# A block of two networks on one core: zeros are multiplied during the first loads, and VectorE adds the first norm's squares

## The chip, the cores and the metric

The kernel runs on one core of a Trainium2 chip. The time is that of the device for one execution, in microseconds (us); of several runs the median is given. A profiled execution also has a span, from the first to the last instruction that the profiler saw.

## The reference, cut to what matters

Input is x with 512 tokens of width 1024, in float32. A first block runs a feed-forward part (ffn1), a token mixer and a second feed-forward part (ffn2); a second block runs two more layers. Only the first part is touched:

```python
def rms_norm(x, g):
    xf = x.astype(jnp.float32)
    y = xf * lax.rsqrt(jnp.mean(xf * xf, axis=-1, keepdims=True) + RMS_EPS)
    return (y * g.astype(jnp.float32)).astype(x.dtype)

def swiglu(x, w_gate, w_up, w_down):
    return (jax.nn.silu(x @ w_gate) * (x @ w_up)) @ w_down

x = x + 0.5 * swiglu(rms_norm(x, ffn1_norm), ffn1_w_gate, ffn1_w_up, ffn1_w_down)
x = x + token_mixer(rms_norm(x, mix_norm), ...)
```

The token mixer holds, beside its products with weights, a recurrence over the tokens that the kernel solves in blocks, with small triangular systems.

## The kernel before, in words

x lies transposed in SBUF: eight tiles `x` of 128 features by 512 tokens. A product in float32 is made of three in the faster type fp32r: each operand is split into a high part and the rest, and `mm3` adds high x high, high x rest and rest x high in one PSUM bank (`pm`). For x the parts are `xh` (ScalarE, with the norm's gain as scale) and `xl` (VectorE), made by `split_scaled`; for a weight tile `raw` of 128 x 1024 they are `wh` (a cast, on ScalarE or VectorE) and `wl` (a subtraction on VectorE), made by `wload`. One weight group against the eight x tiles is 24 matmuls of 128x512. The norm's factor is applied after the product, so TensorE can start before the norm is known.

`rms` first makes the eight pairs of xh and xl, then calls `sumsq`: ScalarE squares each x tile (`sq`, the first into `acc`), and the seven others are added to `acc` one by one, on GpSimd. `fold` sums `acc` over the partitions by two matmuls with a matrix of ones (`rones`, a cast of a part of the constants `cst`), and `rsqrt` makes `rstd` of it, with ScalarE's function Sqrt.

In `ffn`, each of the 22 column groups takes a gate group (`ffn_g`) and an up group (`ffn_u`) of weights. Beside that, `put_low` loads weights of a later part (here `w_in` of the mixer), makes their `wl` and stores it in DRAM (`low`), to be loaded again when it is needed. Every load and store is issued by SyncE, in one queue in order. `raw` has three buffers, `wh` and `wl` four each, so that a load waits until an older one has been split.

The order on every engine is not that of the code. `Rec` records all operations, and `schedule` plans the whole program with a cost per operation, a state of ScalarE's tables, of the buffers and of TensorE's clock; at each moment an engine takes the ready operation with the lowest number, which is its place in the code plus a bias (`late`, 60, for the operations of the norm). An operation that may run on two engines (a cast, some additions) is given to one of them. Any change to the first operations can thus move operations everywhere behind them. `emit` writes the program in the planned order.

In the mixer, `inverse32` solves the small triangular systems of one pair of heads: two stores of `ab` into DRAM (`dab`), eight loads `n` of their diagonal blocks in another layout, 31 steps on VectorE that make `u`, four stores of it (`dtt`), and two loads (`TT`) of the result for TensorE. There are four pairs.

Of the kernel before, what the change touches and what calls it, by code (L numbers as in the profile page):

```python
# [643 lines left out]
class Net:  # L644
    def __init__(self, tc, a, ctx, wbufs=(3, 4, 4), slots=76):
        self.tc, self.a = tc, a
        self.nc = self.rec = Rec(tc.nc)
        self.cp = ctx.enter_context(tc.tile_pool(name="cst", bufs=1))
        self.wp = ctx.enter_context(tc.tile_pool(name="wgt", bufs=1))
        self.wbufs = dict(zip(("raw", "wh", "wl"), wbufs))  # L650
        self.tp = ctx.enter_context(tc.tile_pool(name="act", bufs=1))
        self.sp = ctx.enter_context(tc.tile_pool(name="small", bufs=4))
        self.pm = ctx.enter_context(tc.tile_pool(name="pmm", bufs=8, space=PSUM))
        self.dp = ctx.enter_context(tc.tile_pool(name="dram", bufs=1, space=bass.MemoryType.DRAM))
        self.n = 0
        self.slots = slots
        self.late = 60
        self.low, self.later, self.behind, self.far = {}, [], 40, None
        nc = self.nc
        self.cst = self.cp.tile([128, _NC], F32, name="cst")  # L660
        self.vec = self.cp.tile([128, _NV], F32, name="vec")
        nc.sync.dma_start(out=self.vec, in_=a["vec"])
        self.load_x(a["xT"])
        nc.sync.dma_start(out=self.cst, in_=a["cst"])
        self.ident = self.c("ident")
        self.cr = {}
        for m in ("ones", "bones"):
            self.cr[m] = self.cp.tile([128, 128], F32R, name="r" + m)
            nc.vector.tensor_copy(self.cr[m], self.c(m))
        self.eps6 = self.cst[:, _COFF["eps"]:_COFF["eps"] + 1]  # L670
        self.epsg = self.cst[:, _COFF["eps"] + 1:_COFF["eps"] + 2]
        self.one = self.cst[:, _COFF["eps"] + 3:_COFF["eps"] + 4]
# [128 lines left out]
        self.nc.vector.scalar_tensor_tensor(l, src, g, h.bitcast(F32), op0=ALU.mult, op1=ALU.subtract)  # L801
        return h, l

    def sumsq(self, gains=None):

        nc = self.nc
        acc = self.T(p="acc")
        for k in range(KT):
            if k == 0:
                q = acc  # L810
            else:
                q = self.T(p="sq")
            if gains is None:
                nc.scalar.activation(q, self.x[k], AF.Square)
            else:
                nc.scalar.activation(q, self.x[k], AF.Square, scale=gains(k))
            if k:
                nc.gpsimd.tensor_tensor(acc, acc, q, ALU.add)
        ps = self.P()
        self.fold(ps, "ones", acc)  # L820
        return ps
# [16 lines left out]
        nc.vector.tensor_scalar(r, r, -0.5 * scale, 1.5, op0=ALU.mult, op1=ALU.add)  # L838
        nc.vector.tensor_tensor(out, out, r, ALU.mult)

    def rms(self, gname):

        xs = [self.split_scaled(self.x[k], self.v(gname, k)) for k in range(KT)]
        self.rec.bias = self.late
        ps = self.sumsq()
        rstd = self.T(p="rstd")
        self.rsqrt(rstd, ps, 1.0 / D, 1e-6)
        self.rec.bias = 0
        return xs, rstd


    def ffn(self, n):
        nc = self.nc
        xs, rstd = self.rms(n + "_norm")
        g0 = 0
        for ch, nk in enumerate((8, 8, 6)):
            hs = []
# [852 lines left out]
    def last_norm(self, hf):  # L1710
# [4 lines left out]
        s0 = slice(256 * hf, 256 * hf + 256)  # L1715
        if hf == 0:

            w = self.sm(1, tag="fw", bufs=1)
            o = A.activation(w, self.one, AF.Sqrt)
            o.deps.append(next(p for p in reversed(self.rec.ops[:-1]) if p.table))  # L1720
        acc, q7 = (self.T(shape=(128, 512), p="sq")[:, 0:256] for _ in range(2))
# [31 lines left out]
    def all(self):  # L1753
# [2 lines left out]
        mix = [("w_in", t) for t in (5, 9, 1, 6, 10, 2, 7, 11, 3, 13, 17, 21, 14, 18, 22, 15, 19, 23, *range(26, 42))]  # L1756
        mix += [("w_out_a", h) for h in range(4)] + [("w_out_b", h) for h in range(4)] + [("w_o", g) for g in range(8)]
        n = len(self.rec.ops)
        self.later = mix
        self.ffn("ffn1")  # L1760

        w = [o for o in self.rec.ops[n:] if o.fn == "dma_start"][:2]
        l = [o for o in self.rec.ops[:n] if o.fn == "dma_start"]
# [31 lines left out]
```

## Time and profile before

| what | value |
|---|---|
| median of 3 runs | 1911.29 us (1911.15 to 1913.51) |
| the profiled execution | 1912.9 us |
| its span | 1911.1 us |
| TensorE busy (PE) | 98% |
| VectorE (DVE) | 70% |
| ScalarE (ACT) | 45% |
| GpSimd (POOL) | 13% |

PE is TensorE's matmuls and PEld its loads of weights, SPq is SyncE's queue that issues DMAs. A busy time is a share of the span; matmuls are pipelined and overlap in the records, so the distance between the starts of two of them tells the pace. A timeline row reads: start, duration, engine, line, operation, out<-in, shape, count, and in brackets the idle time before it and what ended that. All operations have one line, that of the function which emits them, so they are told apart by the names of their tiles.

### The profile page before, as it was taken

How to read it: one execution, taken by the hardware profiler on the slowest of the kernel's cores; microseconds unless marked ns; L12 is line 12 of the kernel's file. 1: busy time of each engine (PE TensorE's matmuls, PEld its weight loads, DVE VectorE, ACT ScalarE, POOL GpSimd, SP SyncE). 2: the span in 40 equal slices, each digit the busy share in tenths (PEclk: the TensorE clock that was granted, in tenths of full speed). 3: DMA queues.
4: the chain of work that ended last, by engine and by line, in shares of the span. 5: the costliest groups of instructions: out<-in, count | busy, mean ns of one | idle time of the engine just before them, and what ended most of it. 6: DMA issues, size and time to landing. Idle time of an engine off the chain costs nothing.

```text
span 1911.1 us, 25539 instructions
## 1 busy us (share of the span) xinstructions
PE 1867.3 (98%) x9756; PEld 1548.5 (81%) x9756; DVE 1334.9 (70%) x2173; ACT 852.7 (45%) x1187; POOL 252.5 (13%) x201
## 2 busy tenths in 40 slices
PE   8999999999999999999999999999999999999998
PEld 6878888878877777788788788788899888888887
DVE  7766655568977873567566567865378985899774
ACT  5333423453333422444334334522245554898671
POOL 3101101212121200411001014220000101000001
PEclk9999999999999999999999999999999999999999
DMA  7898884526633533658878774412221225555552
GB/s 257 280 318 287 303 281 158 150 97 203 190 125 111 157 129 118 221 180 297 284 262 295 271 272 131 127 58 73 84 86 45 67 67 198 184 185 204 198 176 100
DMA packets 128810, 345.36 MB, mean 181 GB/s; under 512 B 32304, under 2 KB 44848, under 8 KB 128688
## 3 DMA queue, kind: packets, MB, share of 16 engines
q1 hardware_dynamic: 128688, 343.74, 53.7%
q8 instruction: 76, 1.25, 0.3%
q14 instruction: 46, 0.38, 0.1%
HBM read 280.25 MB, written 63.44 MB: 180 GB/s over the span
## 4 chain that ended last, share of the span: by engine, by line
PE 71%; DVE 11%; DMA 11%; ACT 3%; issue 2%; POOL 1%; SPq 1%; DVEq 0%; ACTq 0%; POOLq 0%
PE pm L551 67%; DVE wl L551 4%; PE pw L551 4%; DMA low<-wl 3%; DMA raw<-o_in 2%; DVE t L551 2%; ACT wh L551 2%; DMA raw<-ffn_d 1%; DMA raw<-ffn_u 1%; DMA raw<-w_in 1%; DVE l L551 1%; DMA n<-dab 1%; DMA raw<-gw 1%; SPq L551 1%; DVE q L551 1%
## 5 line engine op out<-in xcount | busy, mean ns | idle before, releaser
L551 ACT CAST wh<-raw 128x1024 fp32r<-128x1024 f32 (+1 forms) x334 | 347.2, 1041 | 678.6 <-PE pm L551 300.7
L551 PE MATMUL pm<-xh,wh 128*128 128x512 f32 x1488 | 584.0, 393 | 9.6 <-ACT xh L551 8.0
L551 PE MATMUL pm<-xl,wh 128*128 128x512 f32 x1488 | 584.1, 393 | 1.9 <-DVE xl L551 1.9
L551 PE MATMUL pm<-xh,wl 128*128 128x512 f32 x1488 | 582.6, 392 | 1.8 <-DVE wl L551 1.8
L551 DVE TENSOR_TENSOR wl<-raw,wh 128x1024 fp32r<-128x1024 f32 (+1 forms) x303 | 383.0, 1266 | 212.1 <-DMA low<-wl 103.6
L551 PEld LDWEIGHTS pm<-xh,wh 128*128 128x128 f32 x1488 | 280.3, 189 | 69.2 <-ACT xh L551 9.1
L551 PE MATMUL pm<-h,wh 128*128 128x512 f32 (+1 forms) x844 | 321.5, 385 | 10.0 <-ACT h L551 6.8
L551 PEld LDWEIGHTS pm<-xl,wh 128*128 128x128 f32 x1488 | 280.5, 188 | 62.4 <-DVE xl L551 5.0
L551 PEld LDWEIGHTS pm<-xh,wl 128*128 128x128 f32 x1488 | 280.4, 188 | 61.6 <-DVE wl L551 4.3
L551 PE MATMUL pm<-l,wh 128*128 128x512 f32 (+1 forms) x844 | 322.2, 384 | 2.6 <-DVE l L551 2.5
L551 PE MATMUL pm<-h,wl 128*128 128x512 f32 (+1 forms) x844 | 321.4, 383 | 0.0
L551 POOL TENSOR_TENSOR t<-t,t 128x512 f32<-128x512 f32 x61 | 95.2, 1561 | 942.2 <-DVE t L551 796.1
L551 PEld LDWEIGHTS pm<-h,wh 128*128 128x128 f32 x844 | 158.2, 188 | 44.3 <-ACT h L551 8.5
L551 PEld LDWEIGHTS pm<-l,wh 128*128 128x128 f32 x844 | 158.4, 188 | 36.5 <-DVE l L551 6.5
L551 PEld LDWEIGHTS pm<-h,wl 128*128 128x128 f32 x844 | 158.5, 188 | 29.8
L551 DVE TENSOR_TENSOR t<-pm,rstd 128x512 f32<-128x512 f32 x146 | 98.7, 684 | 19.8 <-PE pm L551 15.8
L551 ACT ACT_TABLE_LOAD x71 | 91.1, 1283 | 21.9 <-DVE s L551 14.9
L551 DVE CAST wh<-raw 128x1024 fp32r<-128x1024 f32 x75 | 54.9, 733 | 50.6 <-PE pm L551 28.7
L551 POOL TENSOR_TENSOR acc<-acc,sq 128x512 f32<-128x512 f32 x42 | 65.6, 1569 | 138.5 <-ACT sq L551 138.1
L551 DVE TENSOR_TENSOR x<-x,pm 128x512 f32<-128x512 f32 (+1 forms) x44 | 27.8, 636 | 68.8 <-PE pm L551 67.3
L551 ACT ACTIVATE t<-t 128x512 f32<-128x512 f32 x100 | 59.8, 626 | 30.5 <-DVE t L551 29.5
L551 DVE TENSOR_TENSOR l<-t,h 128x512 fp32r<-128x512 f32 x84 | 58.7, 706 | 6.3 <-ACT h L551 5.0
(245 smaller groups left out, 2127.5 us busy)
## 6 DMA issues: line engine op xcount, KB each, us to landing
low<-wl SPq DMA_DIRECT2D x106, 512.0 KB, 3.8
wl<-low SPq DMA_DIRECT2D x106, 512.0 KB, 3.7
raw<-w_in SPq DMA_DIRECT2D x76, 512.0 KB, 4.8
raw<-o_in SPq DMA_DIRECT2D x64, 512.0 KB, 4.5
raw<-ffn_g SPq DMA_DIRECT2D x44, 512.0 KB, 4.0
raw<-ffn_u SPq DMA_DIRECT2D x44, 512.0 KB, 5.0
raw<-ffn_d SPq DMA_DIRECT2D x32, 512.0 KB, 5.2
raw<-o_out SPq DMA_DIRECT2D x32, 512.0 KB, 4.6
```

The lines of the kernel that those rows point to most:

```text
L551: o.ins = getattr(getattr(self.nc, o.eng), o.fn)(*o.args, **o.kw)
```

## The change

At the start of the program GpSimd fills a tile `z` of 128x512 with zeros; ScalarE takes the Sqrt of its first column (so that the table with Sqrt is loaded then), and TensorE multiplies `z` by itself twenty times into one PSUM bank that nobody reads. In ffn1 the seven additions of squares go to VectorE instead of GpSimd, and the bias of that norm's operations is 100 instead of 60. The rest renames a small tile.

```diff
+        z = self.T(F32R, p="z")
+        nc.gpsimd.memset(z.bitcast(F32), 0.0)
+        nc.scalar.activation(self.sm(1, tag="fw", bufs=1), z[:, 0:1].bitcast(F32), AF.Sqrt)
+        ps = self.P()
+        for _ in range(20):
+            nc.tensor.matmul(ps, z[:, 0:128], z, start=True, stop=True)
...
-    def sumsq(self, gains=None):
+    def sumsq(self, gains=None, adds="gpsimd"):
...
-                nc.gpsimd.tensor_tensor(acc, acc, q, ALU.add)
+                getattr(nc, adds).tensor_tensor(acc, acc, q, ALU.add)
...
-    def rms(self, gname):
+    def rms(self, gname, adds="gpsimd"):
...
-        ps = self.sumsq()
+        ps = self.sumsq(adds=adds)
...
-        xs, rstd = self.rms(n + "_norm")
+        xs, rstd = self.rms(n + "_norm", "vector" if n == "ffn1" else "gpsimd")
...
-            w = self.sm(1, tag="fw", bufs=1)
+            w = self.sm(1, tag="fx", bufs=1)
...
+        late, self.late = self.late, 100
         self.later = mix
         self.ffn("ffn1")
+        self.late = late
```

The first place is TensorE's beginning. Before:

```order
L551 MATMUL pm_116<-xh_84,wh_114 128x512
L551 MATMUL pm_116<-xl_85,wh_114 128x512
L551 MATMUL pm_116<-xh_84,wl_115 128x512
L551 MATMUL pm_116<-xh_86,wh_114 128x512
L551 MATMUL pm_116<-xl_87,wh_114 128x512
L551 MATMUL pm_116<-xh_86,wl_115 128x512
```

And now; the numbers of all tiles are higher by 3, so pm_119 is the former pm_116, the first gate group:

```order
L551 MATMUL pm_74<-z_72 128x512 x20
L551 MATMUL pm_119<-xh_87,wh_117 128x512
L551 MATMUL pm_119<-xl_88,wh_117 128x512
L551 MATMUL pm_119<-xh_87,wl_118 128x512
L551 MATMUL pm_119<-xh_89,wh_117 128x512
L551 MATMUL pm_119<-xl_90,wh_117 128x512
L551 MATMUL pm_119<-xh_89,wl_118 128x512
```

The twenty matmuls stand in front; behind them the order of the first group is the old one.

The second place is VectorE's beginning, where it splits x and the first two weight tiles (wl_115 and wl_119). Before:

```order
L551 TENSOR_TENSOR wl_115<-raw_113,wh_114 128x1024
L551 SCALAR_TENSOR_TENSOR xl_85<-x_74,vec,xh_84 128x512
L551 SCALAR_TENSOR_TENSOR xl_87<-x_75,vec,xh_86 128x512
L551 TENSOR_TENSOR wl_119<-raw_117,wh_118 128x1024
L551 SCALAR_TENSOR_TENSOR xl_89<-x_76,vec,xh_88 128x512
L551 SCALAR_TENSOR_TENSOR xl_91<-x_77,vec,xh_90 128x512
L551 SCALAR_TENSOR_TENSOR xl_93<-x_78,vec,xh_92 128x512
L551 SCALAR_TENSOR_TENSOR xl_95<-x_79,vec,xh_94 128x512
L551 SCALAR_TENSOR_TENSOR xl_97<-x_80,vec,xh_96 128x512
L551 SCALAR_TENSOR_TENSOR xl_99<-x_81,vec,xh_98 128x512
L551 CAST rones<-cst 128x128
L551 CAST rbones<-cst 128x128
```

And now:

```order
L551 SCALAR_TENSOR_TENSOR xl_90<-x_78,vec,xh_89 128x512
L551 TENSOR_TENSOR acc_103<-acc_103,sq_104 128x512
L551 TENSOR_TENSOR wl_122<-raw_120,wh_121 128x1024
L551 SCALAR_TENSOR_TENSOR xl_92<-x_79,vec,xh_91 128x512
L551 SCALAR_TENSOR_TENSOR xl_94<-x_80,vec,xh_93 128x512
L551 SCALAR_TENSOR_TENSOR xl_96<-x_81,vec,xh_95 128x512
L551 SCALAR_TENSOR_TENSOR xl_98<-x_82,vec,xh_97 128x512
L551 SCALAR_TENSOR_TENSOR xl_100<-x_83,vec,xh_99 128x512
L551 SCALAR_TENSOR_TENSOR xl_102<-x_84,vec,xh_101 128x512
L551 TENSOR_TENSOR acc_103<-acc_103,sq_105 128x512
L551 CAST rones<-cst 128x128
L551 CAST rbones<-cst 128x128
```

One addition stands ahead of the second wl, one behind the last xl; three follow behind rbones, ahead of the third wl, and one each behind the third and the fourth.

The third place is SyncE's queue in the mixer, where the third pair of heads ends its solve (u_1034, TT_1036) and the fourth begins (ab_1163). Before:

```order
L551 DMA dtt_728<-u_1034 32x8x32 x4
L551 DMA dab_727<-ab_1163 128x4x128
L551 DMA TT_1036<-dtt_728 128x4x128
L551 DMA TT_1037<-dtt_728 128x4x128
L551 DMA raw_1250<-w_out_a 128x1024
L551 DMA dab_727<-ab_1166 128x4x128
```

And now:

```order
L551 DMA dtt_731<-u_1037 32x8x32
L551 DMA dab_730<-ab_1166 128x4x128
L551 DMA dtt_731<-u_1037 32x8x32
L551 DMA dab_730<-ab_1169 128x4x128
L551 DMA dtt_731<-u_1037 32x8x32
L551 DMA n_1170<-dab_730 32x16x32
L551 DMA dtt_731<-u_1037 32x8x32
L551 DMA n_1170<-dab_730 32x16x32 x3
L551 DMA n_1171<-dab_730 32x16x32
L551 DMA TT_1039<-dtt_731 128x4x128
L551 DMA TT_1040<-dtt_731 128x4x128
L551 DMA n_1171<-dab_730 32x16x32 x3
```

The fourth pair's stores and loads, whose loads stood six rows further down, are now mixed into the third pair's.

## Rows read from the trace of the kernel before

**Rows 1.** The page: busy time, share of the span and instructions of each engine.
```profile
PE 1867.3 (98%) x9756; PEld 1548.5 (81%) x9756; DVE 1334.9 (70%) x2173; ACT 852.7 (45%) x1187; POOL 252.5 (13%) x201
```

**Rows 2.** Stretches: length, busy PE, PEld, DVE, ACT, POOL, granted clock, DMA share, GB/s.
```profile
0.00:20.00 20.00, 11.07 (x32) 6.69 (x33) 12.90 (x12) 13.56 (x21) 7.53 (x9) 1.00 0.79 283
20.00:100.00 80.00, 80.00 (x354) 66.24 (x353) 64.04 (x64) 34.07 (x41) 14.43 (x10) 1.00 0.78 268
100.00:350.00 250.00, 247.55 (x1087) 203.31 (x1087) 151.78 (x170) 85.06 (x91) 26.27 (x16) 1.00 0.76 256
350.00:800.00 450.00, 436.35 (x2837) 345.46 (x2836) 328.10 (x768) 173.36 (x275) 86.37 (x82) 1.00 0.48 152
600.00:700.00 100.00, 95.78 (x815) 74.70 (x813) 86.85 (x252) 37.25 (x67) 14.75 (x17) 1.00 0.34 107
800.00:1900.00 1100.00, 1090.24 (x5440) 925.17 (x5439) 773.42 (x1146) 546.02 (x760) 117.92 (x85) 1.00 0.50 168
```

**Rows 3.** The timeline of the first 30 us.
```profile
2.59 0.43 SPq L551 DMA_DIRECT2D raw<-ffn_u  x1
...
5.45 1.23 DVE L551 TENSOR_TENSOR wl<-raw,wh 128x1024 fp32r<-128x1024 f32 x1
5.89 1.28 ACT L551 ACT_TABLE_LOAD   x1 [5.89 <-DMA x<-xT]
...
7.95 0.80 PE L551 MATMUL pm<-xh,wh 128*128 128x512 f32 x1 [7.95 <-ACT xh L551]
...
9.46 1.03 ACT L551 CAST wh<-raw 128x1024 fp32r<-128x1024 f32 x1
...
9.76 0.63 PE L551 MATMUL pm<-xh,wh 128*128 128x512 f32 x1
...
10.19 0.63 PE L551 MATMUL pm<-xl,wh 128*128 128x512 f32 x1
...
11.96 7.18 DVE L551 SCALAR_TENSOR_TENSOR xl<-x,vec,xh 128x512 fp32r<-128x512 f32 x6
...
13.10 0.40 PE L551 MATMUL pm<-xh,wl 128*128 128x512 f32 x1
...
20.30 0.22 DVE L551 CAST rbones<-cst 128x128 fp32r<-128x128 f32 x1
20.44 5.67 DVE L551 TENSOR_TENSOR wl<-raw,wh 128x1024 fp32r<-128x1024 f32 x3
...
23.66 0.39 PE L551 MATMUL pm<-xh,wh 128*128 128x512 f32 x1
```

**Rows 4.** The tile x: its loads and xl; its landing; the landing of the first ffn_u.
```profile
L551 SPq DMA_DIRECT2D x<-xT x8: 424/492/707, 1.7 to 6.1; - x8
L551 DVE SCALAR_TENSOR_TENSOR xl<-x,vec,xh x8: 740/751/1787, 7.9 to 17.4; 128x512 fp32r<-128x512 f32 x8
DMA to landing us min/median/max: 4.2/6.7/6.8
DMA to landing us min/median/max: 6.2/6.2/6.2
```

**Rows 5.** Groups by form, first 30 us: count, busy us, mean ns, idle before.
```profile
L551 POOL TENSOR_TENSOR acc<-acc,sq 128x512 f32<-128x512 f32 x7 | 11.1, 1580 | 12.4 <-ACT sq L551 12.1
L551 DVE TENSOR_TENSOR l<-acc,h 128x512 fp32r<-128x512 f32 x1 | 0.7, 678 | 0.0
```

**Rows 6.** Groups of GpSimd over the whole span.
```profile
L551 POOL MEMSET zb<- 128x512 f32 x8 | 4.1, 527 | 10.5 <-PE pw L551 8.8 <-DVE aT L551 1.6
```

**Rows 7.** The timeline of SyncE's queue in the mixer.
```profile
635.74 1.80 SPq L551 DMA_DIRECT2D dtt<-u  x4
...
644.64 0.98 SPq L551 DMA_DIRECT2D TT<-dtt  x2
...
652.01 10.18 SPq L551 DMA_DIRECT2D n<-dab  x8
```

**Rows 8.** Two stretches at the mixer's start, columns as in rows 2.
```profile
395.00:398.40 3.40, 1.84 (x7) 1.16 (x7) 3.37 (x6) 3.16 (x4) 0.00 (x0) 0.99 0.04 6
398.40:401.80 3.40, 3.40 (x9) 2.67 (x8) 0.59 (x1) 0.00 (x0) 0.00 (x0) 0.50 0.41 148
```

## What is predicted, and how it is worked out

> **What bounds the kernel now.** I read the busy table first: TensorE is busy 98% of the span, the next engine 70% [rows 1]. So the end moves only with TensorE's idle time, its clock and its number of matmuls. The table by stretches then says where it idles [rows 2]: 8.9 us in the first 20, nothing from 20 to 100, 2.5 from 100 to 350 (all of the first ffn's rest), 13.7 from 350 to 800 (the token mixer; 4.2 of them from 600 to 700), 9.8 in the 1100 us after that. From 20 to 100 it does 354 matmuls in 80.00 us, 0.226 us apiece, without a wait. There a matmul that starts earlier ends everything behind it earlier, and what is won before 20 us is carried on, unless something else becomes late.
>
> The start, in order of time [rows 3]: ScalarE waits for the first x until 5.89, loads its table for 1.28 us, and only then makes the first xh; TensorE begins at 7.95. Its first matmuls start 0.43 us apart (9.76, 10.19), about twice the 0.226, and a record lasts 0.63 us there but 0.40 at 13.10: that is the 1.2 GHz level after complete idleness, and then the 2.4 GHz one. (The granted clock of the stretch reads 1.00 all the same [rows 2]; here the spacing tells it.) VectorE makes the last six xl from 11.96 in 7.18 us, 1.2 each, though the median xl takes 0.75 and only some 1.79 [rows 4]: GpSimd adds squares beside it, seven times 1.58 us [rows 5]. The first two weight groups, gate and up, are 48 matmuls; the 49th starts at 23.66. That time is my yardstick.
>
> **The change part by part.** *Table.* The load of 1.28 us leaves the path. The next one, ahead of the norm's Sqrt, is gone too, since the first table is now the one with Sqrt; nobody but the norm waits for it, and TensorE goes on for tens of us without the norm, so it counts nothing. Not all 1.28 us come through: the next limit is the landing of the data. The up weights are issued at 2.59 and land 6.2 us later [rows 3, 4], at 8.8; ScalarE's cast of them (1.03) began at 9.46 and can now begin at 8.85. The eight x tiles are issued from 1.7 to 6.1 and land 4.2 to 6.8 us later [rows 4], the last by 12.9. So ScalarE's chain moves forward by 0.6 us, not by 1.28.
>
> *Squares.* GpSimd's seven adds cost 1.58 us each on it [rows 5] and go to VectorE, at the 0.68 us of the like `l<-acc,h` [rows 5]: 7 x 0.68 = 4.8 us more for VectorE. It gets back about as much: six xl at 0.67 to 0.75 instead of 1.2 (some 3 us) and, of the three wl from 20.44 in 5.67 us, what they take over 1.23 each (2.0) [rows 3]. All but two of the adds stand behind the last xl, and the first stands in a gap: VectorE waits there for the cast of the up weights. That GpSimd's adds are what stretches them is read from the two kinds of xl side by side; the bounds below take in that it is not.
>
> *The path anew, from these rows.* Cast of the up weights done at 9.9; its wl (1.23, as at 5.45) at 11.15; six xl at 0.67 to 0.75: the last at 15.2 to 15.6. TensorE: nine matmuls can run before that wl, the tenth needs it. From 11.2 on, 39 more at 0.23 give the 49th at 20.2. By the other limit: the last xl feeds the 28th, 21 more at 0.23 are 4.8 us, 20.0 to 20.4. Both agree: 20.2 against 23.66, a gain of **3.5 us**. About 0.6 of it is the table, the rest is the clock and the xl together; they can't be told apart by adding, since each alone would leave the other as the limit.
>
> *Warm-up.* A 128x512 memset on GpSimd takes 0.53 [rows 6]; with the preamble ahead of it I take 1.4 for TensorE's start, an estimate (SyncE's first issues stand at 1.7 to 2.6 [rows 3, 4]). Twenty matmuls at 0.43 are 8.6 us, until 10.0, if the clock does not rise meanwhile. In the trace the level had changed by 13.10, at most 5.1 us after the first matmul at 7.95 [rows 3]; taken as 4.7, the same delay from 1.4 gives eleven at 0.43 and nine at 0.226, until 8.2. Real work would have been ready at 6.65, but the first nine matmuls need only be done by 11.2, and 8.2 plus nine at 0.23 is 10.3. So the warm-up hides under the wait for the up weights; that is its cover, and it has about 1 us to spare.
>
> *Bounds of the gain.* Below, by the clock: it stays low until about 12.7 as today; warm-up until 10.0, six real matmuls by 12.7, 42 at 0.23: 49th at 22.3, gain 1.3. Below, by the xl: they take 7.18 us as now, with the last at 18.3 and the 49th at 23.1: gain 0.5. Above: only the landing of the last x counts: 12.9, + 0.78 for its xh (7.95 less 5.89 and 1.28), + 0.75 for its xl, = 14.4, + 4.8 = 19.2, gain 4.5. I take 3.5, which uses single rows at each step.
>
> *Does it survive to 350?* Between the last xl and the third group's wl VectorE now has four adds and two small casts, 4 x 0.68 + 0.4: it begins at 18.3 and ends at 19.5; TensorE needs it at 20.7. The loads behind it wait for the buffers that these wl empty; the three wl that now run from 20.44 to 26.1 begin 2.1 us earlier and run 2 us shorter, so the loads move by 2 to 4 us, the later ones by more. The DMA share is 0.78 in that stretch [rows 2], so the transfers have room to move along. I count nothing. The norm itself comes later by its bias of 100, but nothing of TensorE's first groups needs it, and VectorE's first chain as a whole ends earlier: nothing either.
>
> *The planner's other moves.* The order is planned anew, and in the mixer it differs in many places, without change of the work. This has no row of its own. Bounds: all 13.7 us that TensorE idles there [rows 2] could go, or as much be added. The nearest row is that of 600 to 700 with its 4.2 us, the stretch in which one pair is solved and the next begun; half of such a stretch may come or go: 0, plus or minus 2.
>
> **Sum.** The profiled execution took 1912.9 us (span 1911.1): 1909.4 after. The median of the runs, 1911.29, is 1.6 below it: **1907.8**, 0.18% faster.
>
> **The rivals.** *(A) The mixer gains too.* In the new order SyncE fetches the fourth pair's dab and n between the third pair's dtt stores, not after them. Before, the eight n are issued from 652.01 for 10.18 us [rows 7], TensorE idling 4.2 us around it. If 3 of these go: 1904.8.
>
> *(B) The same move costs.* The third pair's TT loads now stand behind two dab stores and five n loads. One n costs 10.18 / 8 = 1.27 us of SyncE, so TT comes at least 5 x 1.27 = 6.4 us after dtt, where now it could follow at once, and later still if ab is late, since the queue waits for it. It decides as soon as TensorE's independent matmuls run out before TT lands; if all 6.4 are lost: 1907.8 + 6.4 = 1914.2, slower than before. Against it: TT was late in the old order too (644.64, where the four dtt from 635.74 took 1.80 us to issue), because dab stood ahead of it.
>
> *(C) The start gains less.* The warm-up overruns by a microsecond (gain 2.6), or the clock falls again between it and the dense work. The trace has a fall after a sparse stretch: 7 matmuls in 3.4 us, and the next 3.4 us are granted 0.50 [rows 8], the 1.2 GHz level; nine matmuls cost 9 x 0.2 = 1.8 us there. Between 8.2 and 11.2 the new kernel has nine matmuls, about as sparse. Then the gain is 3.5 - 1.8 = 1.7. Time: 1911.3 - 2.6 = 1908.7 to 1911.3 - 1.7 = 1909.6. The Trainium skill (TensorE: Matmul & The Clock Gate, section HAM oscillation) has it that gaps between bursts bring the slow clock back and that the change to full speed is then paid again; by that page the second half of this rival is the rule, and the stretch of [rows 8] agrees with it. Whether three us with nine matmuls are such a gap no row tells.
>
> *(D) It doesn't do what it says.* The zeros are multiplied but the clock has not risen by 11 us, or the xl stay long for another reason: the two lower bounds above, 1911.3 - 1.3 = 1910.0 and 1911.3 - 0.5 = 1910.8.
>
> **How the numbers follow.** Forecast 0.48, around 1907.8 (1906.6 to 1909.0); A 0.22 (1903.5 to 1906.6); B 0.12 (1910 to 1915); C and D together 0.18 (1908.7 to 1910.8). A bound of 0.2%, 3.8 us, is about what a measurement of this kernel can tell from no change: 1907.5. Half of the forecast's own chance lies below it, with A 0.46 faster. Slower needs 1915.1, the far end of B: 0.05. The rest, 0.49, is within. The range goes from 1904.0 to 1911.5; it leaves out A's tail and the dearer half of B.
>
> **What would show it.** Right: xh at 5.9; six xl in about 4.1 us; matmuls 0.23 apart from the first real one; the 49th real one at 20.2; idle from 20 to 100 still nil. Wrong: warm-up matmuls beyond 10; a wait of TensorE for wl between 20 and 100; more than 16 us idle from 350 to 800, above all at TT; a half-clock stretch before 20.

## The result, and the profile after

In one job on one chip, five runs of each: the changed kernel takes 1925.78 us (1915.98 to 1928.62), the kernel before 1911.39 (1911.15 to 1916.64). The ratio is 1.0058, with an interval of 1.0039 to 1.0078: slower, where 0.18% faster was forecast. A second job gave 1923.04 against 1912.88, 1.0044 (1.0028 to 1.0061). The profiled execution took 1927.12 us, with a span of 1925.1; that is 14.2 us above the one of before.

The page of the changed kernel, as rows 1:

```profile
PE 1878.7 (98%) x9776; PEld 1559.0 (81%) x9776; DVE 1324.4 (69%) x2171; ACT 857.7 (45%) x1194; POOL 241.8 (13%) x196
```

The shares alone say nothing: all but VectorE's 69% are the old ones. The stretches of rows 2 (same columns, without the one from 600 to 700) say more:

```profile
0.00:20.00 20.00, 18.61 (x69) 14.76 (x70) 14.28 (x21) 14.56 (x22) 0.73 (x5) 1.00 0.78 283
20.00:100.00 80.00, 80.00 (x355) 66.30 (x354) 64.42 (x67) 31.77 (x38) 13.29 (x7) 1.00 0.82 286
100.00:350.00 250.00, 242.78 (x1051) 199.77 (x1050) 147.67 (x162) 84.71 (x90) 20.98 (x15) 0.98 0.74 249
350.00:800.00 450.00, 432.94 (x2814) 341.95 (x2813) 316.36 (x756) 174.02 (x274) 87.96 (x83) 0.99 0.46 145
800.00:1900.00 1100.00, 1088.40 (x5364) 920.65 (x5363) 771.11 (x1133) 550.13 (x763) 116.26 (x83) 0.99 0.50 170
```

TensorE has 37 matmuls more in the first 20 us (20 of them zeros), 36 fewer from 100 to 350, 23 fewer from 350 to 800. So the start gained, and the loss begins behind 100 us. The two tables also tell its kind. Behind 20 us TensorE waits 45.0 us in all, against 34.9 before: 10.1 more. It is busy 1860.1 us there against 1856.2, though 17 matmuls fewer are left to do, which are worth 3.8 us: the same work takes 7.7 us longer. Together these 17.8 us are the lead that was won and lost again (3.8) and the 14.0 by which the span is longer. The slower work is that at half the clock: in the trace's clock rows the stretches granted 0.50 between 20 and 1800 us add up to 34.1 us, and to 10.2 in the kernel before.

**The start went as predicted.** From its timeline, as rows 3:

```profile
0.73 1.28 ACT L551 ACT_TABLE_LOAD   x1 [0.73 <-PEq L1790]
1.31 7.37 PE L551 MATMUL pm<-z 128*128 128x512 f32 x20 [1.31 <-POOL z L551]
6.18 0.72 ACT L551 ACTIVATE xh<-x,vec 128x512 fp32r<-128x512 f32 x1 [3.95 <-DMA x<-xT]
10.68 4.06 DVE L551 SCALAR_TENSOR_TENSOR xl<-x,vec,xh 128x512 fp32r<-128x512 f32 x6
19.84 0.39 PE L551 MATMUL pm<-xh,wh 128*128 128x512 f32 x1
```

The table is loaded at 0.73, the zeros run from 1.31 to 8.68, six xl take 4.06 us where they took 7.18, and the 49th real matmul starts at 19.84 instead of 23.66.

**A yardstick by stage.** A matmul `pm<-h,rones`, the fold of a norm, stands six times in the program. The first is that of ffn1's own norm; the second marks the start of the mixer, the third that of ffn2, the fourth lies in the second block. The second and the third, in the timeline of TensorE of the kernel before and then of the changed kernel:

```profile
383.73 0.39 PE L551 MATMUL pm<-h,rones 128*128 128x512 f32 x1
...
835.43 0.39 PE L551 MATMUL pm<-h,rones 128*128 128x512 f32 x1
```

```profile
388.56 0.39 PE L551 MATMUL pm<-h,rones 128*128 128x512 f32 x1
...
845.14 0.39 PE L551 MATMUL pm<-h,rones 128*128 128x512 f32 x1
```

With the fourth (1203.64 and 1217.01), after against before is 3.82 us ahead at the 49th matmul, 4.8 behind at the mixer's start, 9.7 behind at its end, 13.4 behind at the fourth fold, 14.0 at the end of the span. By stage: start -3.8, rest of ffn1 +8.6, mixer +4.9, ffn2 and what follows it up to the fourth fold +3.7, the rest +0.6.

**The first place of the loss.** Until 101 us the lead of 3.8 us holds. ffn1 works its groups in chunks of eight; where the down products of the first chunk need `h` and `l` of the eighth up group, the kernel before waits 0.71 and 0.61 us:

```profile
102.22 0.68 DVE L551 TENSOR_TENSOR t<-pm,rstd 128x512 f32<-128x512 f32 x1
...
105.91 0.73 PE L551 MATMUL pm<-h,wh 128*128 128x512 f32 x2 [0.71 <-ACT h L551]
...
107.25 0.50 PE L551 MATMUL pm<-l,wh 128*128 128x512 f32 x1 [0.61 <-DVE l L551]
```

The same place in the timeline of the changed kernel:

```profile
102.48 1.23 DVE L551 TENSOR_TENSOR wl<-raw,wh 128x1024 fp32r<-128x1024 f32 x1 [1.85 <-DMA low<-wl]
103.62 0.68 DVE L551 TENSOR_TENSOR t<-pm,rstd 128x512 f32<-128x512 f32 x1
103.88 1.04 ACT L551 CAST wh<-raw 128x1024 fp32r<-128x1024 f32 x1 [2.62 <-DMA raw<-ffn_d]
104.45 1.27 POOL L551 TENSOR_TENSOR t<-t,t 128x512 f32<-128x512 f32 x1 [12.43 <-DVE t L551]
105.15 1.04 ACT L551 CAST wh<-raw 128x1024 fp32r<-128x1024 f32 x1 [0.23 <-DMA raw<-w_in]
106.11 0.61 ACT L551 CAST h<-t 128x512 fp32r<-128x512 f32 x1
106.77 0.79 PE L551 MATMUL pm<-h,wh 128*128 128x512 f32 x1 [5.17 <-ACT h L551]
```

VectorE's `t` stands behind a wl that waits for a store `low` to empty its buffer; GpSimd waits for `t`; ScalarE's `h` stands behind two casts that wait for loads. TensorE waits 5.17 us, and the stretch behind the wait is granted half:

```profile
105.75:109.16 3.41, 2.39 (x6) 1.91 (x7) 2.83 (x3) 0.97 (x2) 0.00 (x0) 0.50 0.93 263
109.16:112.57 3.41, 3.41 (x10) 2.63 (x9) 1.92 (x2) 2.09 (x2) 0.00 (x0) 0.50 0.95 305
```

The level is 1.2 GHz (0.50) after a wait in which TensorE did nothing. From 106.77 to 112.57 it starts 16 matmuls where 25 or 26 fit at 0.226 us, so the slow clock costs some 2.2 us; with the wait that is 7.4, against 1.3 of waiting in the kernel before. The lead of 3.8 has become a lag of 2.5. At the end of the second chunk, near 240 us, it waits 1.96 us for `h` (0.90 in the kernel before) and lags 4.85 behind that.

### The profile page after: what moved, and what is told of

It is laid out like the page before. It is cut to its first block, busy times and chain, and to the rows that moved or that the text cites. A ratio compares the mean times of both kernels' runs of the same rounds, so it can differ in the third digit from the quotient of the medians.

```text
span 1925.1 us, 25573 instructions
## 1 busy us (share of the span) xinstructions
PE 1878.7 (98%) x9776; PEld 1559.0 (81%) x9776; DVE 1324.4 (69%) x2171; ACT 857.7 (45%) x1194; POOL 241.8 (13%) x196
## 4 chain that ended last, share of the span: by engine, by line
PE 66%; DMA 13%; DVE 11%; ACT 5%; issue 3%; SPq 1%; POOL 1%; DVEq 0%; ACTq 0%; POOLq 0%
PE pm L551 62%; DVE wl L551 5%; PE pw L551 4%; DMA low<-wl 3%; ACT wh L551 3%; DMA raw<-w_in 3%; DMA raw<-o_in 2%; DVE t L551 2%; DMA raw<-ffn_d 1%; SPq L551 1%; DMA raw<-w_out_a 1%; DMA raw<-gw 1%; DVE l L551 1%; DVE q L551 1%; DVE x L551 1%
## 5 line engine op out<-in xcount | busy, mean ns | idle before, releaser
L551 ACT CAST wh<-raw 128x1024 fp32r<-128x1024 f32 (+1 forms) x341 | 354.2, 1041 | 695.5 <-PE pm L551 298.4
L551 DVE CAST wh<-raw 128x1024 fp32r<-128x1024 f32 x68 | 48.3, 710 | 42.6 <-PE pm L551 31.1
L551 POOL TENSOR_TENSOR acc<-acc,sq 128x512 f32<-128x512 f32 x35 | 54.5, 1566 | 126.1 <-ACT sq L551 126.0
L551 DVE TENSOR_TENSOR q<-u,n 128x128 f32<-128x128 f32 (+15 forms) x188 | 62.9, 354 | 4.4 <-DMA n<-dab 2.5
```

The source lines that it names most:

```text
L551: o.ins = getattr(getattr(self.nc, o.eng), o.fn)(*o.args, **o.kw)
```

## The experiments

Each was timed against the kernel before in the same job; a ratio is over that kernel. Its medians by job were 1911.4 to 1915.7 and its single runs 1907 to 1922, so the three runs shown at first, 2.4 us apart, had understated the spread. Times by stage are from one trace each, of one execution, and the jobs ran on different chips.

### Which part of the change, and is it the order?

The planner replans everything behind an edit, so the new start and the new order were separated. First the new start alone, with the old order kept row by row behind it: the plan is made without the 22 new operations, and these and the seven adds are put in by hand.

```diff
+        head, r.ops = r.ops[:22], r.ops[22:]
...
+        q = r.schedule()
...
+        r.order = head + q
+        r.emit(self.tc)
```

> The changed kernel's start (zeros, early table, the seven additions on VectorE) with the order of the kernel before behind it: the planner is run without the new operations, and they are put in by hand; no other row of any engine moves. Theory 'order' (the new start is good for 3.8 us and lasts; the loss is made by the new plan): the 49th real matmul at 19.8 to 20.0 us, the lead of 3.8 us still there at 100, 350 and 800 us, waits of TensorE as before (1.3 us near 100, 13 to 15 from 350 to 800), time 1911.3 - 3.8 = 1907.5, between 1906.5 and 1909. Theory 'collision' (the loads and splits cannot come as early as TensorE now needs them, in any order): a wait of about 5 us near 102 us as in the changed kernel, the lead gone behind it, time 1911 or more.

Measured: 1916.76 against 1913.67, 1.0011 (0.9996 to 1.0025). The 49th matmul starts at 21.57. It is later than 19.84 since the first gate weights, issued at the same time, land later in this run:

```profile
6.53 0.70 DVE L551 CAST wh<-raw 128x1024 fp32r<-128x1024 f32 x1 [6.53 <-DMA raw<-ffn_g]
...
11.77 4.06 DVE L551 SCALAR_TENSOR_TENSOR xl<-x,vec,xh 128x512 fp32r<-128x512 f32 x6
```

At the first chunk's end it waits about as the kernel before does:

```profile
104.41 0.73 PE L551 MATMUL pm<-h,wh 128*128 128x512 f32 x2 [1.06 <-ACT h L551]
...
105.86 0.51 PE L551 MATMUL pm<-l,wh 128*128 128x512 f32 x1 [0.72 <-DVE l L551]
```

The loss is gone with the old order, but so is the gain. Each theory has one half of it: as 'order' has it, there is no wait of 5 us; as 'collision' has it, the time is not below 1911. Second the new order alone: the changed kernel's plan with the memset, the Sqrt and the zeros not written out.

```diff
+        r.order = [o for o in r.order if o.seq > 21]
```

> The order of the changed kernel on every engine, but the fill with zeros, the early Sqrt and the twenty matmuls of zeros are left out when the planned order is written (they feed nothing). Theory 'order': the wait of about 5 us at the end of the first chunk stays, though TensorE comes there later (then near 104), and so do the waits of the mixer; the time is that of the changed kernel plus what the warm-up gave, 1925.8 + 2 = 1928, between 1922 and 1931. Theory 'collision': with the late start the new order is as good as the old, no wait over 2 us near 104, time 1911 to 1914.

Measured: 1919.11, 1.0027 (1.0015 to 1.0039): the order alone, with VectorE's adds, loses. TensorE starts late here (49th matmul at 21.74) and yet waits 5.82 us for `h` at 109.33, where the changed kernel waits 5.17: so that wait comes with the order, not with the early start. The time is below the 1922 to 1931 that was expected: with the new start the same order took 1.0044 and 1.0058 in other jobs, so that start seems to be worth nothing here. Third and fourth, parts of the change with their own plans, both with the squares on GpSimd and the bias at 60: table and zeros, and the table without the zeros.

```diff
-        xs, rstd = self.rms(n + "_norm", "vector" if n == "ffn1" else "gpsimd")
+        xs, rstd = self.rms(n + "_norm", "gpsimd")
...
-        late, self.late = self.late, 100
+        late, self.late = self.late, 60
```

> Zeros and early table alone, planned anew: the additions of squares stay on GpSimd and the norm's bias stays 60. Its plan has the changed kernel's order in the mixer, but at the end of the first chunk of ffn1 the order of the kernel before. Theory 'order': no wait over 2 us near 102; the start gains less than 3.8 because the last six xl stay long (49th real matmul at 21 to 23); the changed kernel's other losses stay, so 1925.8 - 6.3 + 1.5 = 1921, between 1916 and 1924. Theory 'collision': a wait of 3 us or more near 103, time 1922 to 1927.

Measured: 1921.03, 1.0034 (1.0022 to 1.0046), as theory 'order' had it.

```diff
-        ps = self.P()
-        for _ in range(20):
-            nc.tensor.matmul(ps, z[:, 0:128], z, start=True, stop=True)
```

> The fill with zeros and the early Sqrt alone, no matmuls of zeros, additions on GpSimd, bias 60, planned anew. Its plan has the changed kernel's order at the end of the first chunk of ffn1 (t of the eighth up group behind two wl on VectorE) and the order of the kernel before in the mixer and behind it. Theory 'order': the start gains 0.5 to 1 us, then a wait of about 5 us near 104 and the half clock behind it cost about 6.3; time 1911.3 - 0.7 + 6.3 = 1917, between 1914.5 and 1918.5. Theory 'collision': TensorE starts hardly earlier, so there is no wait over 2 us near 104, time 1910 to 1912.

Measured: 1922.41, 1.0044 (1.0031 to 1.0058). A fill of 0.53 us and an activation on one column, ahead of everything, cost 8.7 us, where 3.2 to 7.2 were expected: nothing in them can take that time, so the new plan does. Here the replanned rows are in ffn1, its chunk ends among them (waits of 4.33 us at 109 and 4.05 at 247), while the mixer's order is the old one but for one row; in the third kernel the chunk ends have the old order and the mixer the new one. The stages go the same way: the rest of ffn1 takes 370.7 us with the table alone and 365.2 with table and zeros, the mixer 451.6 and 457.5; the kernel before has 360.1 and 451.7. That the third kernel's ffn1 also takes 5.1 us more, with the old order at the chunk ends and waits there of 2.10, 0.67 and 1.37 us, is not explained by those rows; its plan differs from the old one in the first 60 us.

The xl of the same two kernels settle what stretched them:

```profile
11.28 7.17 DVE L551 SCALAR_TENSOR_TENSOR xl<-x,vec,xh 128x512 fp32r<-128x512 f32 x6
```

```profile
11.80 7.17 DVE L551 SCALAR_TENSOR_TENSOR xl<-x,vec,xh 128x512 fp32r<-128x512 f32 x6
```

With the squares on GpSimd six xl take 7.17 us, zeros or not; with them on VectorE 4.06 to 4.07 in the changed kernel and in the first two experiments. The Trainium skill (SBUF — State Buffer, Who interferes with whom) has it that a VectorE instruction with two inputs in SBUF contends with a GpSimd instruction that reads SBUF; the traces agree, at 3.1 us for these six.

### Is it the rows at the chunk ends?

If TensorE's wait at 101.6 is the loss, the cure is to put the late rows back. In the changed kernel `t` goes ahead of the cast and the two wl in front of it, `h` ahead of its two casts and `l` ahead of one wl:

```diff
+        u, h, l = self.ends[0]
+        q = self.rec.schedule()
+        self.rec.order = self.ahead(q, [(u, 3), (h, 2), (l, 1)])
```

> The changed kernel with three rows moved at the end of the first chunk of ffn1, all other rows and all other engines as they are: on VectorE the eighth group's t (up product times rstd) goes ahead of one cast and two wl, and its l ahead of one wl; on ScalarE its h goes ahead of two wh. Theory 'order' (these rows make the wait of 5.17 us and the half clock behind it, 6.3 in all): TensorE idles under 2 us near 102, the lead after it is 2 to 6 us better than in the changed kernel, and the median is 4 to 7 us below the changed kernel's of the same job; the mixer's loss stays. Theory 'collision' (loads and splits can't come earlier): the wait only moves to the next weights, and 3 us or more are still lost between 95 and 125 us.

Measured: 1925.77, 1.0057 (1.0039 to 1.0076), the changed kernel's own ratio. The wait did go, and came back one chunk later:

```profile
103.92 0.50 PE L551 MATMUL pm<-l,wh 128*128 128x512 f32 x1 [0.78 <-DVE l L551]
...
242.15 0.80 PE L551 MATMUL pm<-h,wh 128*128 128x512 f32 x1 [6.39 <-ACT h L551]
```

The lag at the mixer's start is the same (388.69). So the rows that were named are where the loss is taken, not what makes it. The same move at both chunk ends, in the first experiment's kernel and in the kernel before:

```diff
+        (u, h, l), (u2, h2, l2) = self.ends[:2]
+        r.order = head + self.ahead(q, [(u, 2), (h, 2), (l, 2), (u2, 1), (h2, 2), (l2, 1)])
```

> The first run's kernel (old order, new start) with t, h and l of the last group moved ahead of the weight splits at the ends of both chunks of ffn1. Theory 'order': the lead of the start (2 to 3.8 us) passes both chunk ends, where the first run lost 1.3 of 2.1; median 1913.7 - 4.5 = 1909, below both kernels. Theory 'collision': the lead is gone by 350 us all the same, and the median is within 2 us of the kernel before of the same job.

Measured: 1913.93 against 1912.88, 1.0001 (0.9988 to 1.0015), not the 1909 of theory 'order'.

> The kernel before with only those rows moved at both chunk ends (no zeros, additions on GpSimd). It tells how much of the previous run's gain is the moved rows' and how much the start's. TensorE idles 1.32 us near 105 and 0.90 near 238 in the kernel before: theory 'order' expects both waits under 0.5 us, median 1.5 to 3 us below the kernel before, and the previous run 2 to 3.5 below this one. Theory 'collision' expects this one equal to the previous run.

Measured: 1915.32, 1.0008 (0.9996 to 1.0021). The lead of the one over the other at the 49th matmul, 2.7 us, is 2.2 at the mixer's start and 2.4 at its end; neither is faster than the kernel before, and by their medians they are 1.4 us apart, within the noise. In both the wait went to the second chunk's end too (2.34, and 1.78 with 0.53, where the kernel before has 0.90). The changed kernel was run again beside them:

> The changed kernel again, beside the three above and on the same chip. The wait of 5 us at the first chunk's end is planned in, so it should be there in this execution as well, with 6 to 7 us lost between 95 and 125 us; median 10 to 13 above the kernel before of the same job. If the wait is under 2 us here, the loss was one execution's and not the order's.

Measured: 1.0044, as said above. The wait is there again (4.11 us at 106.36), and so is the start (49th at 20.49); the rest of ffn1 takes 364.1 us, the mixer 460.5.

### Is it the loads and splits beside ffn1?

What is late at the chunk ends waits for loads, and for stores `low` that empty buffers; from 105 to 240 us VectorE's wl wait for those, in the table of waits (engine and line, what it waits for: us, times, longest), in the changed kernel and then in the kernel before:

```profile
DVE wl L551 <- DMA low<-wl: 25.1, 17, 4.6
```

```profile
DVE wl L551 <- DMA low<-wl: 11.4, 9, 4.1
```

This sum by itself does not tell what TensorE loses: the first experiment's kernel has 20.5 us of it, in 17 waits, and no wait of TensorE over 1.5 us.

So the work of `put_low` beside ffn1 was left out, in the kernel before, in the first experiment's kernel and in the changed one: 49 of its 50 tiles are not loaded, cast, subtracted or stored, and the mixer reads the one that is left.

```diff
+        gone = set(self.gone)
+        self.rec.order = [o for o in self.rec.order if o not in gone]
```

> The kernel before without the side work of ffn1: of the 50 weight tiles of later parts that are loaded, split and stored beside ffn1, 49 are left out (load, cast, subtraction, store), in an otherwise unchanged order; the later loads of their rests all read the one that is kept, so those later products are not the reference's. Control for the next two. Theory 'loads' (in ffn1 the loop of loads, splits and stores sets TensorE's time at the chunk ends): no waits of TensorE from 20 to 350 us beyond those of the last group's own chain, some 2 us less than the kernel before at 350. Theory 'order': the same 2 us at the chunk ends as before.

> The same omission in the first run's kernel (old order, new start). Theory 'loads': with the loop slack, the lead of the start (2 to 3.8 us over the control) is still there at 350 us and, the order being the same, at the end: 2 to 4 us less than the control in the median. Theory 'order' would have had that in the first run already and expects no change of the difference to its control: within 1.5 us of it.

> The same omission in the changed kernel. Theory 'loads' for ffn1 and 'order' for the mixer: the lead of the start passes the first chunk's end (the wait of 4 to 5 us there shrinks to under 2, since most of the splits that stood ahead of the last group's t are gone) and the second, so at 350 us it stands 2 to 4 us ahead of the control; the mixer then takes 5 to 7 us more than the control's, and the end is 2 to 6 us later than the control's. If ffn1's loss were the order's alone, 4 us or more would still be lost at the chunk ends.

Measured, in this order: 1911.60, 1910.80 and 1914.54 against 1915.66; 0.9975 (0.9965 to 0.9986), 0.9968 (0.9958 to 0.9979) and 1.0003 (0.9988 to 1.0017). From 100 to 240 us in the three, columns as in rows 2:

```profile
100.00:240.00 140.00, 140.00 (x620) 115.95 (x619) 63.17 (x79) 25.20 (x29) 19.62 (x10) 1.00 0.32 98
```

```profile
100.00:240.00 140.00, 140.00 (x619) 115.95 (x618) 62.21 (x79) 25.20 (x29) 18.16 (x10) 1.00 0.32 102
```

```profile
100.00:240.00 140.00, 140.00 (x620) 115.91 (x619) 59.40 (x75) 27.31 (x31) 18.04 (x10) 1.00 0.31 98
```

TensorE never waits, and the DMA share is 0.31 to 0.32 (0.86 in the first experiment). The mixer's first fold stands, in the same order, at

```profile
380.84 0.39 PE L551 MATMUL pm<-h,rones 128*128 128x512 f32 x1
```

```profile
377.31 0.39 PE L551 MATMUL pm<-h,rones 128*128 128x512 f32 x1
```

```profile
377.20 0.39 PE L551 MATMUL pm<-h,rones 128*128 128x512 f32 x1
```

The lead of 3.5 to 3.6 us is whole, in the new order as in the old one: from the 49th matmul on all three take 356.4 us. At the end little of it is left: the second kernel is 0.8 us below the first by the medians, where theory 'loads' had 2 to 4. With the side work the kernel before takes 3.7 us more than that, the changed one 12.3 (7.7 when it was run again). This is shown: it is the loads, splits and stores beside ffn1 that eat the lead, and they cost more in the new order. Which of them does it is not shown, since the transfers, the work on VectorE and ScalarE and the use of the buffers were all taken away at once.

The rest of the loss is in the mixer, even here: 464.8 us in the third kernel, 451.2 and 454.5 in the others. That trace overstates it: its execution took 1920.82 us, 6.3 above the kernel's median, and it has a wait of 3.39 us for `h`, at 513, which no other trace of the new order has. By the medians the new order is 2.9 to 3.7 us above the old one. In the changed kernel's own trace the mixer has seven waits of TensorE of 0.9 us or more, 8.6 us in all, where the kernel before has four, 4.2 in all. The longest was tried. In the changed kernel the weights `w_out_a` stand in SyncE's queue behind eight `n` of the fourth pair and the third pair's two `TT`, and TensorE waits for their cast:

```profile
652.38 0.31 SPq L551 DMA_DIRECT2D n<-dab  x1
653.27 2.75 SPq L551 DMA_DIRECT2D n<-dab  x4
656.13 0.97 SPq L551 DMA_DIRECT2D TT<-dtt  x2
657.15 1.56 SPq L551 DMA_DIRECT2D n<-dab  x3
658.75 0.60 SPq L551 DMA_DIRECT2D raw<-w_out_a  x1
...
664.08 1.04 ACT L551 CAST wh<-raw 128x1024 fp32r<-128x1024 f32 x1 [1.11 <-DMA raw<-w_out_a]
...
665.18 0.80 PE L551 MATMUL pm<-h,wh 128*128 128x512 f32 x1 [2.50 <-ACT wh L551]
```

The kernel before issues that load at 645.68, ahead of all `n`. The experiment puts it there:

```diff
+        w = next(o for o in sp[n[-1]:] if o.kw["in_"].tensor.name == "w_out_a")
+        self.rec.order = self.ahead(q, [(w, sp.index(w) - n[-8])])
```

> The changed kernel with one row moved in SyncE's queue: the load of w_out_a that stands behind the eight loads n of the fourth pair in the mixer goes ahead of them, as in the kernel before. Theory 'order' (rival B's mechanism, with another load as its victim): the wait of 2.2 to 3.0 us for that weight near 662 is gone, the half clock behind it is shorter, and the mixer from its start to 800 us takes 3 to 5 us less; median 3 to 4 below the changed kernel. Rival: the pair's own chain on VectorE is as late, TensorE waits for TN or l in its place, and the mixer takes as long as before within 1 us.

Measured: 1923.29 against 1915.66, 1.0038 (1.0026 to 1.0051). The load goes out at 648.04 and the wait shrinks from 2.50 to 1.10 us:

```profile
661.14 0.80 PE L551 MATMUL pm<-h,wh 128*128 128x512 f32 x1 [1.10 <-ACT wh L551]
```

What is left is no longer the load's: it has landed by 652.4, and the cast begins at 660.04, behind ScalarE's `h` of the same matmul and a copy. The mixer takes 454.0 us, 2.6 less than in the changed kernel's trace, but other traces of the new order have 454.1 to 464.8, and the changed kernel was not run in this job (1.0044 and 1.0058 in the others); so the row seems worth two or three us at most and is not the whole of it.

### Does the clock take the lead back later?

With the old order the lead was gone by the end even where ffn1 kept it. One suspect was left: the half-clock stretch behind a wait, which may come again at a later wait and make up for arriving early. Zeros were multiplied in the two waits of the later parts, before the last h of ffn2 (20) and before the second block's fold (12), in the kernel before and in the first experiment's:

```diff
+        for at, out, n in ((up, bank, 20), (fold, fold.args[0], 12)):
+            z = [self.rec.tensor.matmul(out[:, 0:384], zk[:, 0:128], zk, start=True, stop=True) for _ in range(n)]
+            i = q.index(at)
+            q[i:i] = z
```

> The kernel before, with matmuls of zeros laid into the two long waits of TensorE behind the mixer: 20 (of 384 columns) ahead of the matmul that waits 4 to 6 us for the last h near 1051, and 12 ahead of the one that waits 2.9 us for the sum of squares near 1203; nothing else moves. Theory 'clock' (a stretch of 3.4 or 6.8 us at 0.50 behind each of these waits costs about half of itself, and takes the gain of an earlier start as often as not): no stretch at 0.50 near 1055 and 1205, the matmuls behind the waits start 0.23 apart at once, and the median is 3 to 5 us below the kernel before. Rival: the zeros run late and delay the waiting matmul, or the clock falls all the same, then within 1.5 us of the kernel before.

> The same zeros in the first run's kernel (old order, new start). Theory 'clock': 3 to 5 us below the kernel before from the two waits, and the start's lead adds what the loads leave of it at 350 us (0 to 2 us): median 4 to 6 below the kernel before, and 0 to 2 below the run above. If the lead after 350 us is lost to something else than the clock, this one is no faster than the run above, or slower as the first run was (by 2 to 3).

Measured: 1913.03 and 1912.41 against 1913.54; 0.9996 (0.9982 to 1.0009) and 0.9995 (0.9984 to 1.0006). The stretch after the first wait, in the kernel before and then with the zeros in it:

```profile
1053.72:1057.13 3.41, 3.12 (x7) 2.20 (x8) 2.66 (x5) 1.28 (x2) 0.00 (x0) 0.50 0.82 314
```

```profile
1053.00:1058.00 5.00, 2.80 (x11) 2.09 (x12) 4.27 (x6) 2.69 (x4) 0.74 (x1) 1.00 0.91 309
```

The clock holds, at 2.4 GHz, and the time is the same within the interval, not 3 to 6 us less. TensorE's timeline there:

```profile
1049.18 3.63 PE L551 MATMUL pm<-zk 128*128 128x384 f32 x20
1054.97 0.50 PE L551 MATMUL pm<-h,wh 128*128 128x512 f32 x1 [2.16 <-ACT h L551]
```

TensorE waits 2.16 us more for `h`, behind the zeros; the real work begins where `h` arrives (at 1054.01 in the kernel before). So the stretches at these two waits are not what takes the lead. But this pair says nothing of the mixer: there no zeros were laid, and the second kernel's lead, 1.4 us at the 49th matmul, was gone at the mixer's start already (385.79 against 385.15).

In the mixer, in the one pair of traces that kept its whole lead through ffn1, the clock does take it. From the second fold to the third, in the kernel before without side work and then in the first experiment's without it, columns as in rows 2:

```profile
380.84:832.01 451.17, 437.17 (x2845) 345.55 (x2843) 321.51 (x759) 167.80 (x268) 86.96 (x81) 1.00 0.46 148
```

```profile
377.31:831.78 454.47, 441.26 (x2844) 349.21 (x2843) 321.18 (x759) 167.69 (x268) 86.78 (x81) 0.99 0.46 147
```

The second waits 0.8 us less (13.2 against 14.0) and is busy 4.1 us longer with the same matmuls. Its clock rows have two stretches at 0.50 in the mixer, 3.4 us from 391.1 and 6.8 from 664.2; the other has none. In the pair with the rows moved at the chunk ends it is the other way round, 3.4 us at 0.50 with the new start and 6.8 with the old one, and there the lead passed the mixer (2.2 and 2.4 us, above).

## Why the prediction was wrong

*Start: right, with some luck.* Gain 3.8 against 3.5. xh at 6.18 (5.9 predicted), six xl in 4.06 (4.1), 49th at 19.84 (20.2), real matmuls 0.23 us apart from the first one on but where they wait for the second wl, zeros until 8.68 (8.2). After thirteen zeros about 0.43 apart the spacing is 0.23, so the clock rose later than it was taken to, by two matmuls, and the cover of 1 us held. The luck is in the size: in the nine traces with the whole new start the 49th matmul stands at 19.80 to 22.71, mean 20.90, and in the four with the whole old one at 23.66 to 24.42, mean 24.05, a gain of 3.2. Rival D is out. Rival C did not come in the changed kernel, where the stretch between the zeros and the dense work kept 2.4 GHz, but it came with the same start in the last experiment, whose 49th matmul is the latest of the nine, at 22.71:

```profile
12.30:15.70 3.40, 3.40 (x9) 2.65 (x10) 3.40 (x6) 3.40 (x7) 0.00 (x0) 0.51 1.02 414
```

That the parts "can't be told apart by adding" is not borne out: the table alone gains 0.2 (49th at 23.47), the adds without table and zeros 1.9 (21.74), table and zeros with GpSimd's adds 1.6 (22.06), and the last two make 3.5 of the 3.8; but these are single traces.

*"Does it survive to 350? ... I count nothing": the step that failed*, +8.6 in the trace, where 0 stood. The prediction argued from a DMA share of 0.78 that the transfers have room, and that VectorE's chain ends earlier. But the share is an average: beside ffn1 a loop of loads, casts, subtractions and stores runs through three `raw` and four `wl` buffers, and without that loop's work TensorE does not wait at a chunk end at all. The `t`, `h` and `l` that TensorE needs stand in the same engines' queues as that work. That the buffers are what holds the loop back is likely from the waits for `low`, and not shown. Of the new order the prediction weighs VectorE's beginning and SyncE in the mixer; the rows of VectorE and ScalarE at the chunk ends, which the replan had also changed, are not in it. Over the traces with side work, the rest of ffn1 takes 364.1 to 370.7 us with the new plan there (six, mean 367.7), 360.1 to 365.2 with the old one (seven, mean 362.3): 5.4 us for the plan, and the two ranges overlap in one trace each. In the old plan, too, some of the lead goes: the three kernels with the early start reach the mixer at 384.35 in the mean, the three late ones with the same order at 385.15, so 0.8 of 2.1 us is left; the single traces lie 3 us apart on either side, so the size is rough. Of the loss in ffn1 a part is the half clock behind the waits (2.2 us at the first chunk's end), which the prediction's term does not hold either.

*"The planner's other moves: 0, plus or minus 2": mis-sized.* The mixer takes 454.0 to 464.8 us in seven traces with the new order, mean 457.7, and 449.4 to 454.5 in nine with the old one, mean 451.1: 6.6 us for the order. Of these 3.9 are waits (17.0 us against 13.1), and the rest goes with the half clock: 10.3 us of TensorE's work at 0.50 in the mean, against 3.4. The figure is rather high, since the executions traced with the new order took 2.9 us more than their kernels' medians, those with the old one 0.3. By the medians of the kernels without side work the changed order is 3.7 us above the old one. The outer bounds of 13.7 held it; the inner ones, half of a 100 us stretch's idle time, had no row behind their sign, and no term for the clock.

*Rival B was right in kind, wrong in its victim.* It had the third pair's TT late behind five `n`, at 1.27 us apiece. The median `n` takes 0.49 us of SyncE before and after; the 10.18 us of the eight hold one of 3.78 and pauses. TT did come behind five `n`, but no wait of TensorE over 0.4 us hangs on it; `w_out_a`, behind all eight, was issued 13 us later than before, and TensorE waited for that. Rival A, the same move as a gain, has the wrong sign.

*The 3.7 us from 835 to 1203 and what is behind.* The order there is the same in all the kernels (but for the zeros of the last two), which take 366.6 to 372.2 us for it whatever their start; the changed kernel's 371.9 and the old 368.2 lie in that spread, so this part of its trace is no effect that is shown.

*The range.* It gave 0.05 to slower, since it held one mechanism with a loss, in one place. A plan redone over 1900 us can lose in every place where two engines wait for each other.

*What stays open.* The old order with the new start, 3.5 us ahead at 377 when the side work is gone (377.31 against 380.84), is 0.2 ahead at the mixer's end (831.78 against 832.01) and 0.8 by the medians. In these two traces the half clock takes it back, as shown above. Whether an early start makes the clock fall, or chance does, is open: in the mixer's traces with the old order, stretches at 0.50 come and go with either start. What the new start is worth by itself is not resolved either: in the four pairs of kernels that differ in the start alone, new less old is +3.1, -1.4, -0.8 and -0.6 us by the medians. And no version is faster than the kernel before: the best with all the work in it are at 0.9995 and 0.9996, with intervals over 1.

## What to carry to other kernels

When a planner or a scheduler stands between an edit and the program, time the edit with the old order frozen, and the new order without the edit; else a table load of 1.28 us seems to cost 9. A lead at the start is worth what is left of it at the next place where loads, splits and stores set the time: find that place first, and look at the rows of all engines there, not at the bounding one alone. An average DMA share of 0.78 did not mean that what TensorE waits for came in time. And a wait costs more than its length where the clock is at half behind it: 7.7 of the 17.8 us lost here were slower work.

## What the runs showed of the hardware that was not expected

*Landing of the first loads.* The first gate load is issued at 1.18 us with the same one load in front of it. The cast that waits for it starts at 4.72 in the kernel before, at 5.95 in the one without side work, whose first loads are the same, at 4.91 in the changed kernel and at 6.53 in the first experiment. That is a spread of 1.8 us in when TensorE's data come, half of the gain that was looked for. These runs were not all on one chip, so whether the chip or the execution makes it is not shown.

*The clock at the start.* In the ten traces with zeros, all of which begin them at 1.31, the spacing becomes 0.23 after 7 to 14 of them.

*The clock after a wait.* The same rows behind the same waits were granted half the clock in one trace and the whole in another. In the kernel before without side work and in the first experiment's without it, TensorE waits 0.38, 0.56 and 1.00 us for the same three weights behind the mixer's first fold; the stretch that begins with the third wait's end has in the one

```profile
394.50:397.90 3.40, 3.40 (x15) 2.78 (x16) 1.58 (x3) 0.81 (x2) 0.00 (x0) 1.00 0.51 157
```

and in the other

```profile
390.90:394.30 3.40, 3.33 (x8) 2.66 (x9) 1.64 (x4) 0.87 (x2) 0.00 (x0) 0.53 0.48 157
```

Eight matmuls where the other has 15: some 1.6 us, and no row of the two tells the reason. The Trainium skill (TensorE: Matmul & The Clock Gate, HAM oscillation) has it that gaps between bursts bring the slow clock back; the traces agree that they may, and show that waits of one length do not settle it.
